# A decoder step on one core: the samples' pages with paired square sums, casts on ScalarE and products with the values four pages at a time

## The chip, the core and the metric

The kernel runs on one core of a Trainium2 chip. Its engines work side by side, each through its own queue of instructions: TensorE (PE in the profile, its weight loads PEld) multiplies matrices into the accumulator memory PSUM; VectorE (DVE), ScalarE (ACT) and GpSimd (POOL) do elementwise work and sums; SyncE (SP) issues transfers. An instruction waits, by semaphores, for what it reads and for the buffer that it writes. The metric is the time of one execution on the device in microseconds (us); lower is better.

## The reference

One step of a one-layer decoder for 512 prompt tokens and 8 samples (one new token each). Attention, a chunk mixer, a convolutional feed-forward part and a gate follow one another; all in fp32. The change touches the samples' attention over the past: 4096 positions for each sample, in 32 pages of 128, found through a page table in a cache of 128-wide latents and 32-wide rope keys. Cut to that:

```python
def keys_nope(c, w_uk, k_norm_w):
    return rmsnorm(jnp.einsum('bkr,rhd->bkhd', c, w_uk), k_norm_w)

def attend(q_nope, q_rope, k_nope, k_rope, c, w_uv, q_pos, k_pos):
    s = (jnp.einsum('bqhd,bkhd->bhqk', q_nope, k_nope)
         + jnp.einsum('bqhd,bkd->bhqk', q_rope, k_rope)).astype(jnp.float32) * SCALE
    s = jnp.where(k_pos[None, :] <= q_pos[:, None], s, -jnp.inf)
    p = jax.nn.softmax(s, axis=-1).astype(c.dtype)
    o_lat = jnp.einsum('bhqk,bkr->bqhr', p, c)
    return jnp.einsum('bqhr,rhd->bqhd', o_lat, w_uv)
```

So the keys of 8 heads are made from each latent and normalised by their own root mean square over 64 values; that is what the sums of squares are for.

## The kernel before, in words

An fp32 product is made of three products of rounded operands: each factor is split into a high part (a cast) and a low part (what the cast left), and `mm3` (L145) issues high by high, high by low, low by high (L146 to L148).

The samples are eight batches, one for each sample, numbered 0 to 7, of 32 pages. Four pages make a group: `s_load_group` (L577) fetches it some groups ahead, with four page transfers on SP's queue (L601) and an indirect transfer of rope keys on POOL (L588). `s_split` (L703) splits a group's latents: the cast (L714, `a<-u` or `a<-w`) runs on ACT for even groups and on DVE for odd ones, the remainder (L130) on POOL.

`s_page` (L718) does one page: six matmuls of 260 columns (256 key values and 4 raw scores, twice) into a pair of PSUM banks, of which there are three pairs. ACT squares the keys out of PSUM into a buffer of 512 (L750, from a pool of three, `Q`) and copies the raw scores (L751), which frees the pair. DVE sums each 64 squares, 512 to 8 values (L752). Every second group, rope scores are made (L740) and copied (L742).

When a batch's last page has been issued, `s_softmax` (L759) appends its steps to a list, and from the fourth page of the next batch on, one step is issued per page: scale the sums (POOL, L792); logarithm, exponential and square on ACT (L770), which give the inverse root y0 and t = y0²; raw scores times y0 (POOL, L796); `newton` on DVE (L157, L158); add (L798); the maximum of each row (L799); TensorE transposes the maxima (`mx_t`, L782); DVE reduces and spreads them (L785, L786); TensorE copies them to all rows (`mx_b`, L789); DVE subtracts (L803); ACT exponentiates; DVE sums (L806). `mx_t` stands in TensorE's queue among the next batch's pages: if the maxima are late, the pages behind it wait.

`s_pv` (L809), after group 5 of the next batch, multiplies the weights with the values: 32 matmuls of 128 columns, page c in column strip c modulo 4 of the array, and one for the new token (L818). `s_out` (L821) copies the result, `s_fin` (L828) adds the strips with a selection matrix and divides by the sum.

The tile framework allots buffers from tagged pools (`U` has 20 buffers of 1040 and `W` 9 of 1024; pages and splits of groups use both, `A` has the split halves) and a scheduler orders each engine's instructions; `tc.issue_after` adds an order. Batch 0's pages run among the prompt's attention blocks, batches 1 to 7 in the loop at L919. In that loop, at group 60 (in batch 7), the prompt's mixer result is split (`split_all`, L931: casts L135 on ACT, remainders L130 `u<-u` on POOL, 128 by 1040). Behind the pages come the output projection and the feed-forward part, which are matmuls with streamed weights.

Of the kernel before, what the change touches and what calls it, by code (L numbers as in the profile page):

```python
# [12 lines left out]
AF = mybir.ActivationFunctionType  # L13
# [9 lines left out]
DN = 64  # L23
# [10 lines left out]
NCONST = 1389  # L34
# [12 lines left out]
def trunk_step(ctx: ExitStack, tc: tile.TileContext, I, O):  # L47
# [68 lines left out]
    sel = take(8)  # L116
    sel_last = take(8)
# [32 lines left out]
    def mm_cols(out, lhsT, rhs):  # L150

        for q in range(0, 128, 32):
            r = nc.tensor.matmul(out[q:q + 32], lhsT[:, q:q + 32], rhs, start=True, stop=True, tile_position=(0, q))  # L153
        return r
# [546 lines left out]
    bst = {}  # L701

    def s_split(n):  # L703
        if n >= 64:
            return
        b, g = n // 8, n % 8
        pv = pages[b][1][g]
        if n < 12:
            t = U(F32R)
            ch, cl = t[:, 0:512], t[:, 512:1024]  # L710
        else:
            ch, cl = A(F32R)[:, 0:512], A(F32R)[:, 0:512]
        raw = pv[:, :, 0:128]
        (nc.vector.tensor_copy if n % 2 else nc.scalar.copy)(u3(ch, 4, 128), raw)  # L714
        subs.append(sub(u3(cl, 4, 128), raw, u3(ch, 4, 128), "g"))
        csp[n] = (ch, cl)

    def s_page(q):  # L718
# [3 lines left out]
        if j == 0:  # L722
            for m in (n + 2, n + 3):
                if m not in csp and (m == n + 2 or m > 12):
                    s_split(m)
            if g == 0:
                ss = up.tile([128, 256], F32, tag="ss", name=nm("ss"), bufs=2)
                raw = up.tile([128, 256], F32, tag="raw", name=nm("raw"), bufs=2)
                sc = up.tile([128, 288], F32, tag="sc", name=nm("sc"), bufs=2)
                nc.gpsimd.memset(sc[:, 264:288], 0.0)  # L730
                nc.vector.tensor_copy(sc[:, 256:264], snall[:, b])
                bst[b] = (ss, raw, sc)
# [16 lines left out]
        sq = Q()  # L749
        squares.append(nc.scalar.activation(u3(sq, 2, 256), ps[:, :, 0:256], AF.Square))  # L750
        nc.scalar.copy(raw[:, c * 8:c * 8 + 8].rearrange("p (a h) -> p a h", a=2), ps[:, :, 256:260])  # L751
        nc.vector.tensor_reduce(ss[:, c * 8:c * 8 + 8], sq.rearrange("p (h d) -> p h d", d=DN), axis=AX.X, op=ALU.add)  # L752
# [6 lines left out]
    def s_softmax(b):  # L759
# [28 lines left out]
        def mx_b():  # L788
# [6 lines left out]
            lambda: act(t, y0, AF.Square),  # L795
# [3 lines left out]
            lambda: nc.vector.tensor_reduce(m1[:, 0:8], s3.rearrange("p c h -> p h c"), axis=AX.X, op=ALU.max),  # L799
            mx_t,  # L800
# [8 lines left out]
    def s_pv(b):  # L809

        scp, psum = bst.pop(b)
        pg = pages.pop(b)[1]
        po = ms()
        for c in range(32):
            q = 32 * (c % 4)
            nc.tensor.matmul(po[q:q + 32, 0:128], scp[:, c * 8:c * 8 + 32], pg[c // 4][:, c % 4, 128:256],  # L816
                             start=(c < 4), stop=(c >= 29), tile_position=(0, q))
        nc.tensor.matmul(po[0:32, 0:128], scp[:8, 256:288], cnew, start=False, stop=True, tile_position=(0, 0))  # L818
        bst[b] = (po, psum)

    def s_out(b):  # L821
        po, psum = bst.pop(b)
        ol = Q()[:, 0:128]
        with tc.issue_after(squares[-1].ins):
            nc.scalar.copy(ol, po[:, 0:128])
# [318 lines left out]
def _layout(inp):  # L1144
# [27 lines left out]
    def col(v):  # L1172
# [14 lines left out]
         np.tile(np.eye(32, 8, dtype=f), (4, 1)), np.tile(np.eye(32, 8, -24, dtype=f), (4, 1))], 1)  # L1187
# [59 lines left out]
```

## Time and profile before

| | |
|---|---|
| time, three runs | 919.24, 922.05, 924.79 us; median 922.05 |
| time of the profiled execution | 920.34 us |
| its span in the profile | 918.6 us |
| mean granted TensorE clock | 0.99 of full speed |
| first square of batch 1 | 206.15 us |
| last square of batch 7 | 420.06 us |

The profile is of one execution. A group row names line, engine, operation, result and source tiles with their shape, count, then busy time and mean ns of one, then idle time ahead of it and what ended that. A timeline row has start, length, engine, line, operation, and in brackets the idle time before it with what ended it. A wait row names who waited, for whom, the total, the count and the longest. A row of a stretch has its length and for each engine busy time and number of instructions, then the granted clock, the share of the DMA engines and GB/s.

### The profile page before, as it was taken

What the parts mean: (1) busy time and instruction counts of PE and PEld (TensorE: products, weight loads), DVE (VectorE), ACT (ScalarE), POOL (GpSimd) and SP (SyncE); (2) the same over time, 40 slices, a digit from 0 to 9 for tenths busy, and PEclk for the clock granted to TensorE, in tenths of its full rate; (3) what the DMA queues carried; (4) which work ended last, traced back from release to release, by engine and by line L of the source; (5) the groups of instructions that cost most, each with busy time, mean ns of one, the idle gap of its engine ahead of it and who ended that gap; (6) DMA issues with size and microseconds to landing.
All of it is one profiled execution on the core that took longest, in us unless ns stands there. A gap on an engine that the chain in (4) does not pass through costs nothing.

```text
span 918.6 us, 20633 instructions
## 1 busy us (share of the span) xinstructions
PE 892.9 (97%) x7799; PEld 846.5 (92%) x7799; DVE 660.2 (72%) x1133; ACT 503.0 (55%) x1188; POOL 204.7 (22%) x208
## 2 busy tenths in 40 slices
PE   7998999999999999989999999999999999999997
PEld 5896878888898888979999999999999999999997
DVE  6579766669999999897668776337776337776775
ACT  6573368777877787864446443224444214455561
POOL 5004841127676667630000000000000000000000
PEclk9998999999999999989999999999999999999999
DMA  6332150352667556314233222322222222323311
GB/s 217 99 96 81 50 182 1 95 161 79 203 183 210 161 162 193 121 31 138 86 100 110 89 86 86 103 89 87 90 93 92 93 92 93 104 85 98 116 58 59
DMA packets 65204, 100.44 MB, mean 109 GB/s; under 512 B 13825, under 2 KB 47754, under 8 KB 65106
## 3 DMA queue, kind: packets, MB, share of 16 engines
q1 hardware_dynamic: 63058, 94.93, 32.3%
q0 software_dynamic: 2048, 4.20, 1.8%
q8 instruction: 62, 1.02, 0.5%
q14 instruction: 36, 0.29, 0.1%
HBM read 95.95 MB, written 3.15 MB: 108 GB/s over the span
## 4 chain that ended last, share of the span: by engine, by line
PE 82%; DVE 7%; ACT 3%; DMA 2%; issue 2%; SPq 2%; POOL 1%; DVEq 0%; ACTq 0%
PE mm L146 24%; PE mm L148 24%; PE mm L147 23%; DVE ss L752 2%; PE ms L816 2%; PE ms L693 2%; SPq L601 1%; POOL xs L280 1%; DMA u<-pages 1%; DVE g L157 1%; DMA a<-xT 1%; PE ms L153 1%; PE mm L678 1%; PE ms L641 1%; PE mm L658 1%
## 5 line engine op out<-in xcount | busy, mean ns | idle before, releaser
L146 PE MATMUL mm<-u,w 128*128 128x260 f32 x1392 | 395.2, 284 | 0.0
L148 PE MATMUL mm<-u,w 128*128 128x260 f32 x1392 | 394.3, 283 | 0.0
L147 PE MATMUL mm<-u,w 128*128 128x260 f32 x1392 | 393.4, 283 | 0.0
L148 PEld LDWEIGHTS mm<-u,w 128*128 128x128 f32 x1392 | 262.0, 188 | 0.3 <-issue 0.2
L147 PEld LDWEIGHTS mm<-u,w 128*128 128x128 f32 x1392 | 262.1, 188 | 0.2
L146 PEld LDWEIGHTS mm<-u,w 128*128 128x128 f32 x1392 | 261.8, 188 | 0.4 <-PE mm L148 0.2
L130 DVE TENSOR_TENSOR w<-wr,w 128x1024 fp32r<-128x1024 f32 (+1 forms) x94 | 112.8, 1201 | 104.2 <-issue 54.3
L752 DVE TENSOR_REDUCE ss<-sq 128x8 f32<-128x512 f32 x256 | 166.6, 679 | 14.1 <-ACT sq L750 12.2
L750 ACT ACTIVATE sq<-mm 128x512 f32<-128x512 f32 x256 | 153.6, 614 | 34.7 <-PE mm L148 21.1
L135 ACT CAST w<-wr 128x1024 fp32r<-128x1024 f32 (+1 forms) x94 | 96.5, 1031 | 138.1 <-PE mm L148 127.3
L146 PE MATMUL mm<-wuk,a 128*128 128x260 f32 x416 | 124.8, 300 | 3.9 <-ACT raw L751 3.4
L148 PE MATMUL mm<-wuk,a 128*128 128x260 f32 x416 | 119.0, 286 | 0.0
L147 PE MATMUL mm<-wuk,a 128*128 128x260 f32 x416 | 118.6, 285 | 0.0
L146 PEld LDWEIGHTS mm<-wuk,a 128*128 128x128 f32 x416 | 79.4, 191 | 7.8 <-ACT raw L751 6.4
L147 PEld LDWEIGHTS mm<-wuk,a 128*128 128x128 f32 x416 | 79.6, 191 | 0.0
L148 PEld LDWEIGHTS mm<-wuk,a 128*128 128x128 f32 x416 | 79.4, 191 | 0.0
L588 POOL DMA_INDIRECT wr<-krT,idx x64 | 62.1, 971 | 11.4 <-issue 6.3
L1059 ACT ACTIVATE a<-abuf,cst 128x512 f32<-128x512 f32 x44 | 35.9, 816 | 39.3 <-DVE abuf L1057 39.2
L1060 DVE SCALAR_TENSOR_TENSOR a<-abuf,cst,a 128x512 f32<-128x512 f32 x44 | 33.1, 752 | 25.4 <-ACT a L1059 25.1
L130 POOL TENSOR_TENSOR a<-u,a 128x512 fp32r<-128x512 f32 x34 | 45.5, 1339 | 25.8 <-ACT a L714 13.0
L751 ACT COPY raw<-mm 128x8 f32<-128x8 f32 x256 | 45.9, 179 | 0.0
L135 ACT CAST u<-a 128x520 fp32r<-128x520 f32 x24 | 14.8, 626 | 43.4 <-DVE a L1098 43.3
(306 smaller groups left out, 1339.3 us busy)
## 6 DMA issues: line engine op xcount, KB each, us to landing
wr<-w_ffi SPq DMA_DIRECT2D x44, 512.0 KB, 3.3
u<-pages SPq DMA_DIRECT2D x152, 128.0 KB, 2.3
w<-pages SPq DMA_DIRECT2D x104, 128.0 KB, 2.4
wr<-w_ffo SPq DMA_DIRECT2D x16, 512.0 KB, 3.3
wr<-w_o SPq DMA_DIRECT2D x8, 512.0 KB, 4.3
wr<-w_pg SPq DMA_DIRECT2D x8, 512.0 KB, 3.2
wr<-w_ffo SPq DMA_DIRECT2D x8, 384.0 KB, 3.4
a<-xT SPq DMA_DIRECT2D x8, 260.0 KB, 7.2
```

Of the source, the lines that this page charges most:

```text
L130: return (nc.vector if eng == "v" else nc.gpsimd).tensor_sub(dl, src, dh.bitcast(F32))
L135: nc.scalar.copy(dh, src)
L146: nc.tensor.matmul(out, lh, rh, start=start, stop=False)
L147: nc.tensor.matmul(out, lh, rl, start=False, stop=False)
L148: return nc.tensor.matmul(out, ll, rh, start=False, stop=stop)
L588: nc.gpsimd.indirect_dma_start(krT[:, g * 128:(g + 1) * 128], None, I["krT"], bass.IndirectOffsetOnAxis(ap=idx.bitcast(U32)[:, b * 8 + g:b ...
L693: nc.tensor.matmul(po[:, 0:256], v[:, ks], pt_[:, k * 256:k * 256 + 256], start=(k == 0), stop=(k == qb))
L750: squares.append(nc.scalar.activation(u3(sq, 2, 256), ps[:, :, 0:256], AF.Square))
L751: nc.scalar.copy(raw[:, c * 8:c * 8 + 8].rearrange("p (a h) -> p a h", a=2), ps[:, :, 256:260])
L752: nc.vector.tensor_reduce(ss[:, c * 8:c * 8 + 8], sq.rearrange("p (h d) -> p h d", d=DN), axis=AX.X, op=ALU.add)
L1059: nc.scalar.activation(c[:, 0:T], a[:, 2:T + 2], AF.Identity, scale=cw[:, m, 2:3], bias=cw[:, m, 3:4])
L1060: nc.vector.scalar_tensor_tensor(c[:, 0:T], a[:, 1:T + 1], cw[:, m, 1:2], c[:, 0:T], op0=ALU.mult, op1=ALU.add)
```

## The change

For batches 1 to 7, the squares of two pages go into the two halves of one `U` buffer, and one reduce sums both, 1024 to 16 values. Batch 0 stays as it was. Casts of all groups from the ninth on (n >= 8) run on ACT. The copy of the new token's score (L731) goes from DVE to POOL, and t = y0² from ACT to a product on POOL. `mx_t` gets one empty step ahead of it. The products with the values take a group of four pages at once, 512 columns with one stationary block of 32 (4 pages by 8 heads), so that the wanted results stand in four diagonal blocks; `s_out` copies all 512 columns, on DVE, and `s_fin` picks the blocks with four selection matrices, 16 matmuls in place of 4. The new token's product moves to the middle. The constants grow from 1389 to 1405 columns.

```diff
-        (nc.vector.tensor_copy if n % 2 else nc.scalar.copy)(u3(ch, 4, 128), raw)
+        (nc.vector.tensor_copy if n % 2 and n < 8 else nc.scalar.copy)(u3(ch, 4, 128), raw)
...
-                nc.vector.tensor_copy(sc[:, 256:264], snall[:, b])
+                nc.gpsimd.tensor_copy(sc[:, 256:264], snall[:, b])
...
-        sq = Q()
+
+        two = b > 0
+        if not two:
+            bsq["t"] = Q()
+        elif j % 2 == 0:
+            bsq["t"] = U()
+        sq = bsq["t"][:, two * (j % 2) * 512:two * (j % 2) * 512 + 512]
...
-        nc.vector.tensor_reduce(ss[:, c * 8:c * 8 + 8], sq.rearrange("p (h d) -> p h d", d=DN), axis=AX.X, op=ALU.add)
+        if not two or j % 2:
+            w = 2 if two else 1
+            nc.vector.tensor_reduce(ss[:, (c + 1 - w) * 8:c * 8 + 8], u3(bsq["t"], 8 * w, DN), axis=AX.X, op=ALU.add)
...
-            lambda: act(t, y0, AF.Square),
+            lambda: nc.gpsimd.tensor_mul(t, y0, y0),
...
             lambda: nc.vector.tensor_reduce(m1[:, 0:8], s3.rearrange("p c h -> p h c"), axis=AX.X, op=ALU.max),
+            None,
             mx_t,
...
-        for c in range(32):
-            q = 32 * (c % 4)
-            nc.tensor.matmul(po[q:q + 32, 0:128], scp[:, c * 8:c * 8 + 32], pg[c // 4][:, c % 4, 128:256],
-                             start=(c < 4), stop=(c >= 29), tile_position=(0, q))
-        nc.tensor.matmul(po[0:32, 0:128], scp[:8, 256:288], cnew, start=False, stop=True, tile_position=(0, 0))
+        for g in range(8):
+            q = 32 * (g % 4)
+            if g == 4:
+                nc.tensor.matmul(po[0:32, 0:128], scp[:8, 256:288], cnew, start=False, stop=False, tile_position=(0, 0))
+            nc.tensor.matmul(po[q:q + 32], scp[:, g * 32:g * 32 + 32], pg[g][:, :, 128:256],
+                             start=(g < 4), stop=(g >= 4), tile_position=(0, q))
...
-        ol = Q()[:, 0:128]
-        with tc.issue_after(squares[-1].ins):
-            nc.scalar.copy(ol, po[:, 0:128])
+        ol = Q()
+        nc.vector.tensor_copy(ol, po)
...
-            mm_cols(pt_[:, 0:8], ol, sel)
+            for j in range(4):
+                mm_cols(pt_[:, 0:8], ol[:, j * 128:j * 128 + 128], sels[j], j == 0, j == 3)
```

The scheduler moves instructions with it. DVE, from the seventh page of batch 4 on (the rows of batch 3's softmax stand between batch 4's reduces; `ss`, `raw`, `sc` are sums, scores and the result). Before:

```order
467 L714 CAST a_4673<-u_4513 128x512
468 L752 TENSOR_REDUCE ss_4531<-sq_4641 128x8
469 L157 SCALAR_TENSOR_TENSOR g_4508<-ss_3910,g_4508 128x256
470 L752 TENSOR_REDUCE ss_4531<-sq_4653 128x8
471 L752 TENSOR_REDUCE ss_4531<-sq_4694 128x8
472 L158 SCALAR_TENSOR_TENSOR raw_3911<-g_4508,raw_3911 128x256
473 L752 TENSOR_REDUCE ss_4531<-sq_4707 128x8
474 L798 TENSOR_TENSOR sc_3912<-sc_3912,raw_3911 128x256
475 L752 TENSOR_REDUCE ss_4531<-sq_4719 128x8
476 L799 TENSOR_REDUCE s_4509<-sc_3912 128x8
```

DVE at the same place, after:

```order
399 L761 TENSOR_REDUCE ss_4399<-u_4481 128x16
400 L157 SCALAR_TENSOR_TENSOR g_4376<-ss_3822,g_4376 128x256
401 L761 TENSOR_REDUCE ss_4399<-u_4503 128x16
402 L158 SCALAR_TENSOR_TENSOR raw_3823<-g_4376,raw_3823 128x256
403 L807 TENSOR_TENSOR sc_3824<-sc_3824,raw_3823 128x256
404 L761 TENSOR_REDUCE ss_4399<-u_4554 128x16
405 L808 TENSOR_REDUCE s_4377<-sc_3824 128x8
```

The cast is gone from between, and from the first newton step to the maximum two paired reduces stand where four single ones stood.

TensorE at the transpose of the maxima in batch 4 (`mm` is a page's PSUM pair, each page six rows). Before:

```order
1746 L146 MATMUL mm_4784<-wuk_563,a_4527 128x260
1747 L147 MATMUL mm_4784<-wuk_564,a_4527 128x260
1748 L148 MATMUL mm_4784<-wuk_563,a_4528 128x260
1749 L782 MATMUL ms_4735<-cst,s_4509 8x128
1750 L146 MATMUL mm_4784<-wuk_563,a_4527 128x260
1751 L147 MATMUL mm_4784<-wuk_564,a_4527 128x260
1752 L148 MATMUL mm_4784<-wuk_563,a_4528 128x260
1753 L146 MATMUL mm_4796<-wuk_563,a_4527 128x260
```

TensorE, after:

```order
1745 L146 MATMUL mm_4625<-wuk_563,a_4395 128x260
1746 L147 MATMUL mm_4625<-wuk_564,a_4395 128x260
1747 L148 MATMUL mm_4625<-wuk_563,a_4396 128x260
1748 L791 MATMUL ms_4623<-cst,s_4377 8x128
1749 L146 MATMUL mm_4637<-wuk_563,a_4395 128x260
1750 L147 MATMUL mm_4637<-wuk_564,a_4395 128x260
1751 L148 MATMUL mm_4637<-wuk_563,a_4396 128x260
```

The transpose stood in the middle of a page, after 14 and a half of batch 4's pages; now it stands after 14.

POOL in batch 7 (`u<-u` rows of 128x1040 are the remainders of the prompt's split, `a<-` rows those of the pages, `raw` the scores of batch 6). Before:

```order
191 L130 TENSOR_TENSOR u_6717<-u_1037,u_6716 128x1040
192 L130 TENSOR_TENSOR a_6470<-w_6297,a_6469 128x512
193 L588 DMA wr_5981<-krT,idx 128x128
194 L796 TENSOR_TENSOR raw_5774<-raw_5774,g_6371 128x256
195 L130 TENSOR_TENSOR a_6537<-u_6376,a_6536 128x512
```

POOL, after:

```order
206 L804 TENSOR_TENSOR g_6107<-g_6107 128x256
207 L805 TENSOR_TENSOR raw_5554<-raw_5554,g_6107 128x256
208 L130 TENSOR_TENSOR a_6265<-u_6112,a_6264 128x512
209 L130 TENSOR_TENSOR a_6323<-u_6187,a_6322 128x512
210 L130 TENSOR_TENSOR a_6373<-w_6250,a_6372 128x512
211 L130 TENSOR_TENSOR u_6429<-u_1036,u_6428 128x1040
212 L130 TENSOR_TENSOR u_6433<-u_1037,u_6432 128x1040
```

Both remainders of the prompt's split now stand behind the scores and behind the last remainder of a page; t stands ahead of the scores.

More of the change, by code (lines that the diff above doesn't have):

```diff
@@ L33 @@
 EPS = 1e-6
-NCONST = 1389
+NCONST = 1405
 NEG = -1.0e30
@@ L115, in trunk_step @@
     row8 = take(272)
-    sel = take(8)
-    sel_last = take(8)
+    sels = [take(8) for _ in range(4)]
+    sel, sel_last = sels[0], sels[3]
     gqk8 = row8[:8, 0:128].rearrange("p (a d) -> p a d", a=2)
@@ L148, in mm3, with mm_cols @@
         return nc.tensor.matmul(out, ll, rh, start=False, stop=stop)
-    def mm_cols(out, lhsT, rhs):
+    def mm_cols(out, lhsT, rhs, start=True, stop=True):
         for q in range(0, 128, 32):
-            r = nc.tensor.matmul(out[q:q + 32], lhsT[:, q:q + 32], rhs, start=True, stop=True, tile_position=(0, q))
+            r = nc.tensor.matmul(out[q:q + 32], lhsT[:, q:q + 32], rhs, start=start, stop=stop, tile_position=(0, q))
         return r
@@ L701, in trunk_step @@
     bst = {}
+    bsq = {}
     def s_split(n):
@@ L1186, in _layout @@
          np.where(np.tril(np.ones((128, 128))) > 0, 0.0, NEG).astype(f), cw.reshape(128, 176), row8,
-         np.tile(np.eye(32, 8, dtype=f), (4, 1)), np.tile(np.eye(32, 8, -24, dtype=f), (4, 1))], 1)
+         *(np.tile(np.eye(32, 8, -8 * j, dtype=f), (4, 1)) for j in range(4))], 1)
     a["pt"] = g["page_table"].reshape(1, 256)
```

## The prediction

> **What bounds the kernel now.** The page's busy table first: it gives engine, busy time, share of the span.
>
> ```profile
> PE 892.9 (97%) x7799; PEld 846.5 (92%) x7799; DVE 660.2 (72%) x1133; ACT 503.0 (55%) x1188; POOL 204.7 (22%) x208
> ```
>
> TensorE is the bound over the whole span, so an edit that only lightens DVE gains where TensorE waits for DVE. The change touches the samples' pages; batches 1 to 7 run from about 206 to 421 us. I cut that stretch at each batch's first square and asked for busy time in each part (columns: length, then PE, PEld, DVE, ACT, POOL busy, granted clock, DMA share, GB/s). Batch 4 stands for batches 1 to 6, which differ little; the last row is batch 7 with what follows it.
>
> ```profile
> 295.48:325.40 29.92, 28.88 (x343) 26.80 (x342) 27.51 (x50) 23.59 (x78) 19.69 (x20) 1.00 0.58 172
> ...
> 385.27:437.00 51.73, 47.51 (x514) 44.16 (x513) 41.97 (x69) 32.15 (x88) 14.76 (x18) 0.93 0.25 86
> ```
>
> In batch 4 TensorE idles 29.92 - 28.88 = 1.04 us, while DVE is busy 27.51 of 29.92: DVE runs almost level with TensorE. Next, batches 4 and 7 cut at the transpose of the row maxima (L782, which belongs to the batch before) and at the last square.
>
> ```profile
> 295.48:307.19 11.71, 10.67 (x97) 9.86 (x96) 11.40 (x20) 10.34 (x33) 9.48 (x9) 1.00 0.71 210
> 307.19:324.81 17.62, 17.62 (x241) 16.35 (x242) 15.52 (x30) 13.06 (x45) 10.10 (x10) 1.00 0.49 147
> 385.27:400.28 15.01, 11.38 (x101) 10.38 (x99) 13.91 (x19) 12.10 (x37) 12.14 (x13) 1.00 0.25 83
> 400.28:420.66 20.38, 20.38 (x228) 19.09 (x229) 17.66 (x30) 14.15 (x44) 1.48 (x3) 0.83 0.24 83
> ```
>
> All of batch 4's idle time lies ahead of the transpose (10.67 of 11.71; behind it 17.62 of 17.62), where DVE is busy 11.40 of 11.71. Batch 7 takes 15.01 to the same place, 3.3 more, and then 20.38 against 17.62, 2.8 more, at a mean clock of 0.83. Shorter windows show the fall:
>
> ```profile
> 398.00:401.00 3.00, 0.78 (x7) 0.73 (x7) 3.00 (x5) 2.10 (x6) 0.81 (x1) 1.00 0.00 0
> 401.00:404.00 3.00, 3.00 (x28) 2.47 (x28) 1.92 (x5) 1.80 (x7) 0.00 (x0) 0.50 0.00 0
> 404.00:407.00 3.00, 3.00 (x14) 2.98 (x15) 2.54 (x6) 1.20 (x6) 0.96 (x1) 0.50 0.00 0
> ```
>
> TensorE is busy 0.78 of 3 us while it waits for the maxima; then the lower of its two levels (1.2 GHz) is granted for over 6 us. Last, the waits by pair, for PEld from 205 to 440 us and for ACT from 204 to 424 us (total, times, longest):
>
> ```profile
> PEld ms L782 <- DVE s L799: 8.3, 8, 2.4
> PEld mm L146 <- ACT raw L751: 6.4, 12, 1.4
> ```
>
> ```profile
> ACT sq L750 <- DVE ss L752: 9.6, 13, 1.5
> ```
>
> TensorE waits for the maxima from DVE, and for ACT's copies of scores. ACT in turn waits for DVE's reduces to free one of three square buffers. Both waits come from DVE's queue.
>
> **The change, part by part.** The costs of single operations, from the groups between 204 and 424 us (busy and mean ns of one stand behind the bar):
>
> ```profile
> L752 DVE TENSOR_REDUCE ss<-sq 128x8 f32<-128x512 f32 x226 | 146.8, 679 | 10.9 <-ACT sq L750 9.0
> L714 DVE CAST a<-u 128x512 fp32r<-128x512 f32 x14 | 12.6, 898 | 0.0
> L731 DVE COPY sc<-snall 128x8 f32<-128x8 f32 x6 | 6.2, 1031 | 2.9 <-PE ms L818 2.9
> L714 ACT CAST a<-u 128x512 fp32r<-128x512 f32 x20 | 12.7, 636 | 0.0
> L770 ACT ACTIVATE g<-g 128x256 f32<-128x256 f32 x16 | 7.7, 480 | 0.1
> L825 ACT COPY sq<-ms 128x128 f32<-128x128 f32 x7 | 2.0, 286 | 0.0
> L816 PE MATMUL ms<-u,sc 128*32 128x128 f32 x264 | 10.3, 275 | 0.0
> L816 PE MATMUL ms<-w,sc 128*32 128x128 f32 x184 | 8.0, 273 | 0.0
> ```
>
> The chain from batch 3's squares to its transpose, in batch 4, by the timeline: first POOL and ACT, then DVE, then two matmuls of the page behind the transpose (which starts at 307.19).
>
> ```profile
> 299.78 1.00 POOL L588 DMA_INDIRECT wr<-krT,idx  x1 [0.15 <-issue]
> 300.79 0.75 POOL L796 TENSOR_TENSOR raw<-raw,g 128x256 f32<-128x256 f32 x1
> 301.97 1.31 POOL L130 TENSOR_TENSOR a<-u,a 128x512 fp32r<-128x512 f32 x1 [0.43 <-PE mm L148]
> ```
>
> ```profile
> 300.00 0.47 ACT L770 ACTIVATE g<-g 128x256 f32<-128x256 f32 x1
> ```
>
> ```profile
> 300.74 1.10 DVE L714 CAST a<-u 128x512 fp32r<-128x512 f32 x1
> 301.76 0.67 DVE L752 TENSOR_REDUCE ss<-sq 128x8 f32<-128x512 f32 x1
> 302.35 1.21 DVE L157 SCALAR_TENSOR_TENSOR g<-ss,g 128x256 f32<-128x256 f32 x1
> 303.48 1.27 DVE L752 TENSOR_REDUCE ss<-sq 128x8 f32<-128x512 f32 x2
> 304.67 0.41 DVE L158 SCALAR_TENSOR_TENSOR raw<-g,raw 128x256 f32<-128x256 f32 x1
> ...
> 306.53 0.61 DVE L799 TENSOR_REDUCE s<-sc 128x8 f32<-128x264 f32 x1
> ```
>
> ```profile
> 307.43 0.28 PE L147 MATMUL mm<-wuk,a 128*128 128x260 f32 x1
> 307.55 0.28 PE L148 MATMUL mm<-wuk,a 128*128 128x260 f32 x1
> ```
>
> *Paired squares.* Sixteen reduces of 1024 replace 32 of 512 per batch. Two single ones in a row took 1.27. No row has one of 1024: twice the single is at most 1.27; at least about 0.8, by the step from L799's 0.61 for 264 elements to 0.67 for 512. I take 1.2, nearest to the pair. That frees little by itself; what it brings is room, since the squares leave the three-buffer pool for the 20 buffers of U, and ACT's wait of 9.6 in all goes.
>
> *Casts on ACT.* The 28 that leave DVE in batches 1 to 7 cost it about 0.9 each, 3.6 per batch; ACT pays 0.636 each, 2.5 per batch, and gives back 0.48 (the Square) and 0.29 (the output copy). ACT goes from 23.6 busy per batch to about 25.4 of some 29.3, so it stays hidden behind TensorE. The copy of the new key's score (1.03) leaves DVE for POOL; POOL is busy 19.7 of 29.9, and nobody waits for it there.
>
> *t on POOL.* The Exp ends at 300.47, but POOL is in its indirect DMA until 300.78 and starts t then. At the price of its neighbour, 0.75, t is ready at 301.53 and the scaled scores at 302.28, 0.74 later than before. Behind them POOL's cast remainders (L130) and its next indirect DMAs are queued; the pages use those a group later.
>
> *DVE's chain.* Without the cast and the reduce that filled DVE from 300.74 to 302.35, the first newton step can start at 301.6. At its row's 1.21, since POOL is multiplying beside it, it would end at 302.8; unstretched it would end near 302.2; I take 302.6. A pair reduce follows (303.8), then newton's second step and the addition, 0.41 each by L158's row (304.6), one pair reduce (305.8) and the maximum (306.4). Before, the maximum ended at 307.14, so this is 0.74 earlier. The transpose stands half a page earlier in TensorE's order, so half a page, three matmuls at 0.12 from start to start (0.36), must still be run behind it. That leaves 0.38. I add 0.27, an estimate, for DVE's backlog that no longer follows behind the transpose (11.40 busy of 11.71 there): 0.65 per batch, 3.9 over batches 1 to 6. Bounds: 0 (newton at its longest and reduces at 1.27) to 2.0, the whole wait of TensorE there (of the first rival's 14.7, the 12.3 left when the longest, 2.4 in batch 7, is taken off, over six batches).
>
> The Trainium skill, "SBUF — State Buffer", section "Who interferes with whom", says that a DVE instruction with two SBUF inputs contends with a GpSimd instruction that reads SBUF, while a reduce does not. By it newton beside POOL's two products would be drawn out, and the casts taken off DVE were drawn out the same way. The trace agrees: 1.21 for newton beside the subtraction, 0.67 for every reduce. Were the rule to let newton start only once POOL's products are through, the sum would be that of the second rival.
>
> *Products with the values.* Eight matmuls of 512 columns replace 32 of 128: the same columns stream. Over seven batches the 448 records (two for each of 32) are busy at most 10.3 + 8.0 = 18.3, 2.6 per batch, where 64 of 0.275 one after another would take 17.6: the four strips already overlap. I count 0, from -0.3 (fewer starts) to +0.3; the sixteen selections, 12 more, go with it. The output copy of 512 on DVE (about 0.6 at a reduce's price) lies behind the chain, and its reader is three pages later.
>
> *Batch 7.* Four rows:
>
> ```profile
> 391.05 2.67 DVE L714 CAST a<-u 128x512 fp32r<-128x512 f32 x1
> ```
>
> ```profile
> 389.75 2.43 POOL L130 TENSOR_TENSOR u<-u,u 128x1040 fp32r<-128x1040 f32 x1
> 394.56 0.98 POOL L796 TENSOR_TENSOR raw<-raw,g 128x256 f32<-128x256 f32 x1
> ```
>
> ```profile
> 400.28 0.27 PE L782 MATMUL ms<-cst,s 128*8 128x128 f32 x1 [2.22 <-DVE s L799]
> ```
>
> POOL's 2.43 of the prompt's own split stands ahead of the scores, and the cast on DVE lasts 2.67. The cast goes to ACT, and the order puts the two splits behind all the pages' work on POOL. Then batch 7 should run like batch 4: 3.3 to the transpose, and with the idle stretch the clock's fall goes too, 2.8. Together 6.1; bounds 1 (the clock falls all the same) to 7. The two splits are late for the output projection after the pages, which waits for nothing on POOL before about 421.
>
> Sum: 3.9 + 6.1 = 10.0. The profiled execution took 920.34 (span 918.6), 1.7 under the median of the three runs, 922.05. So 910.3 against the former, and **912.0** against the median.
>
> **The rivals.**
>
> *All waits go* (chance 0.13). If the paired reduces cost near 0.8, or newton isn't drawn out, the maxima come before TensorE asks. PEld's waits in the table, 8.3 + 6.4 = 14.7, vanish, and with them at least 3.0 of lost clock (half speed from 401 to 407): -17.7, 904.4. For it: DVE loses about 7 of 27.5 per batch. Against it: the chain is a series of operations that depend on each other, and POOL's two products stand in it before DVE can help.
>
> *The chain starts later* (0.17). If newton's two inputs make it wait out POOL's products and the subtraction behind them (1.31), each transpose comes 1.3 later than forecast: +0.65 per batch in place of -0.65, +3.9; batch 7 keeps 4.8. Sum -0.9: 921.1. For it: newton's stretch to 1.21 and t's added 0.75. Against: DVE has half its queue to catch up with.
>
> *ACT becomes the bound* (0.06), the slower side. ACT gets 28 x 0.636 = 17.8 and gives back 7 x (0.48 + 0.29) = 5.4. It decides if ACT has no slack between squares: a cast between two squares then holds the copy that frees the PSUM pair, and TensorE waits at a page's start. At full price, +12.4, without the steady gain and with batch 7's 6.1: +6.3, 928.4. For it: TensorE already waits 6.4 for that copy. Against: ACT is busy 23.6 of 29.9, and three PSUM pairs absorb one cast of 0.64.
>
> *Batch 7 still stalls* (0.12). ACT now casts the prompt's splits too; if its squares get late there and the clock falls again, 1 of the 6.1 remains: -4.9, 917.2.
>
> **How the numbers follow.** The forecast has 0.52. About 0.5% (4.6 us) is what a measurement of this kernel can tell from no change. Faster by more than that: forecast, the first rival, and half of the last, which sits on the line (917.4): 0.71. Within: the second rival and the other half, 0.23. Slower: ACT, 0.06. The range, 903 to 921, takes in the first rival, the bounds of the steady term and the last rival; it leaves out ACT's case and about half of the second rival.
>
> **What would show it.** In the profile after: no wait of ACT's squares for DVE; DVE busy near 21 per batch; batches 1 to 6 at about 29.2; the transpose some 11.0 behind the first square in batch 7 as in batch 4; granted clock 1.00 from 400 to 410; reduces of 1024 near 1.2. Wrong if the transpose's wait for DVE is as long as before (second rival), if TensorE's waits for ACT's copies grow (third), or if batch 7 still takes 15 us to its transpose.

## The result, and the profile after

| | before | changed |
|---|---|---|
| median of 9 runs | 920.97 us | 925.49 us |
| lowest to highest | 919.24 to 924.79 | 922.38 to 930.29 |
| ratio to before, 95% interval | | 1.0046 [1.0029, 1.0062] |
| span of the profiled execution | 918.6 | 928.5 |

The change made the kernel slower by half a per cent. A second timing of the same kernel gave 1.0020 [1.0005, 1.0035]. The profiled execution of the changed kernel is the longest of its nine; a second profile (below, e_repeat) has a span of 918.4. So the parts that both profiles show are the kernel's, and the part that only one shows is marked.

The batches of the changed kernel, each from its first square to the next one's, the last from batch 7's first square on (length, then PE, PEld, DVE, ACT, POOL busy, granted clock, DMA share, GB/s):

```profile
208.38:242.75 34.37, 31.17 (x319) 28.11 (x318) 22.92 (x29) 25.46 (x80) 22.29 (x24) 0.90 0.49 143
242.75:280.33 37.58, 34.19 (x319) 29.82 (x318) 26.36 (x30) 25.26 (x81) 20.02 (x22) 0.86 0.43 124
...
310.60:340.82 30.22, 28.78 (x319) 25.82 (x318) 24.86 (x30) 24.47 (x80) 20.09 (x22) 1.00 0.52 154
...
401.31:453.00 51.69, 48.98 (x502) 43.43 (x501) 43.35 (x56) 34.67 (x89) 17.59 (x17) 1.00 0.41 137
```

Batches 1 and 2 are 34.37 and 37.58 long, against 29.47 and 29.87 before, and the clock's mean in them is 0.90 and 0.86. Batches 3 to 6 take 30.2 to 30.3 each, where they took 29.9 to 30.0 and 29.3 was forecast. In batch 7 the clock no longer falls: 1.00 where 0.93 stood; from its first to its last square it takes 29.2 where it took 34.8. The difference of the two spans, +9.9, by parts: 2.2 late at batch 1's first square, +4.9 in batch 1, +7.7 in batch 2, +1.2 in batches 3 to 6 together, -5.6 in batch 7, -0.5 behind. The first 2.2 are not in the second profile, whose batch 1 starts at 205.40.

What TensorE's weight loads wait for in the whole span of the changed kernel:

```profile
PEld ms L791 <- DVE s L808: 10.6, 8, 3.6
...
PEld ms L828 <- issue: 6.7, 8, 0.8
...
PEld ms L798 <- DVE s L795: 4.5, 5, 0.9
PEld mm L146 <- ACT raw L758: 3.5, 3, 2.3
```

The wait for the maxima is longer than before (10.6 against 8.3), and behind it stands one that was not there: L798, the copy of the maximum to all rows, waits for DVE's spread L795. The 0.8 ahead of each of the eight products of the new token (L828), now in the middle of the others, is idle time of the weight load alone: TensorE's own waits have no such row. The wait for ACT's score copies has almost halved (6.4 before).

Batch 4 of the changed kernel, cut at the transpose of the maxima and at the copy of the maximum to all rows (columns as above):

```profile
310.60:321.12 10.52, 9.80 (x95) 9.41 (x93) 9.32 (x11) 10.38 (x35) 9.30 (x10) 1.00 0.53 158
321.12:324.92 3.80, 3.08 (x36) 2.69 (x36) 3.77 (x5) 2.60 (x10) 2.24 (x2) 1.00 0.40 119
```

TensorE idles 0.72 ahead of the transpose, where it idled 1.04 before: 0.32 less. Between the transpose and the copy it idles another 0.72, where it had no idle time before. The timeline shows why. Before, DVE and then PE from the maximum's end (307.14) on:

```profile
307.06 1.26 DVE L752 TENSOR_REDUCE ss<-sq 128x8 f32<-128x512 f32 x2
308.25 0.27 DVE L785 TENSOR_REDUCE s<-ms 8x1 f32<-8x128 f32 x1
...
309.04 0.21 DVE L786 TENSOR_SCALAR s<-cst,s 8x8 f32<-8x8 f32 x1
```

```profile
309.66 0.38 PE L789 MATMUL ms<-s,ones 8*128 8x8 f32 x2
```

The changed kernel, DVE:

```profile
316.53 0.94 DVE L157 SCALAR_TENSOR_TENSOR g<-ss,g 128x256 f32<-128x256 f32 x1
317.40 1.21 DVE L761 TENSOR_REDUCE ss<-u 128x16 f32<-128x1024 f32 x1
...
320.44 0.62 DVE L808 TENSOR_REDUCE s<-sc 128x8 f32<-128x264 f32 x1
320.98 2.34 DVE L761 TENSOR_REDUCE ss<-u 128x16 f32<-128x1024 f32 x2
323.23 0.27 DVE L794 TENSOR_REDUCE s<-ms 8x1 f32<-8x128 f32 x1
323.54 1.33 DVE L795 TENSOR_SCALAR s<-cst,s 8x8 f32<-8x8 f32 x1
```

POOL and PE at the end of that stretch:

```profile
323.57 1.28 POOL L130 TENSOR_TENSOR a<-w,a 128x512 fp32r<-128x512 f32 x1 [1.35 <-ACT a L715]
```

```profile
324.92 0.38 PE L798 MATMUL ms<-s,ones 8*128 8x8 f32 x2 [0.72 <-DVE s L795]
```

The maximum (L808) ends at 321.06, 10.46 behind the batch's first square at 310.60; before, it ended 11.66 behind. So the chain up to there gained 1.2. Then two paired reduces of 2.34 together stand ahead of the maximum's second reduce (L794), where two single ones of 1.26 stood; it starts 12.63 behind the first square, against 12.77 before. And the spread, an operation on 8 by 8 elements, takes 1.33 where it took 0.21: it ends with POOL's subtraction, which began beside it and took 1.28. The copy to all rows starts at 324.92, 14.32 behind the first square against 14.18 before. All of the 1.2 is gone.

Batch 2 of the changed kernel, where newton is longest: POOL, then DVE, then PE.

```profile
249.22 0.75 POOL L805 TENSOR_TENSOR raw<-raw,g 128x256 f32<-128x256 f32 x1
249.92 1.29 POOL L130 TENSOR_TENSOR a<-u,a 128x512 fp32r<-128x512 f32 x1
```

```profile
249.31 2.20 DVE L157 SCALAR_TENSOR_TENSOR g<-ss,g 128x256 f32<-128x256 f32 x1 [0.60 <-POOL g L804]
251.43 1.21 DVE L761 TENSOR_REDUCE ss<-u 128x16 f32<-128x1024 f32 x1
252.56 1.48 DVE L158 SCALAR_TENSOR_TENSOR raw<-g,raw 128x256 f32<-128x256 f32 x1
```

```profile
256.21 0.38 PE L791 MATMUL ms<-cst,s 128*8 128x128 f32 x1 [3.39 <-DVE s L808]
```

Newton starts beside POOL's second product and ends 0.30 behind the subtraction that follows it without a gap (249.92 + 1.29 = 251.21). Its second step meets the next subtraction and takes 1.48, where it took 0.41 in batch 4. TensorE waits 3.39 ahead of the transpose. In batch 4 newton starts beside the same product; but there POOL pauses 0.16 ahead of the subtraction, and newton takes 0.94. This holds in every profile of this case: all eight newtons beside a product that a subtraction followed without a gap took 2.15 to 2.20, and all those where the gap was 0.06 to 0.18 took 0.94 to 0.95. The granted clock around it:

```profile
254.00:258.00 4.00, 1.79 (x8) 1.49 (x9) 3.97 (x7) 1.72 (x6) 0.88 (x1) 0.71 0.76 228
258.00:262.00 4.00, 4.00 (x30) 3.47 (x29) 1.96 (x3) 2.08 (x8) 1.28 (x1) 0.50 0.13 41
```

TensorE is busy 1.79 of 4 us, and then the lower level is granted: what batch 7 did before, batch 2 does now.

Last, what SP's page loads wait for between 180 and 290 us, before, and then in the changed kernel:

```profile
SPq L601 <- PE ms L816: 23.1, 2, 16.7
```

```profile
SPq L601 <- DVE ss L761: 17.5, 5, 7.6
```

A load waits for the buffer that it is to fill. Before, the longest of these waits were for the products that read the old pages; now the most is for paired reduces, since squares take buffers of U, which pages need.

### The profile page after: what moved, and what is told of

Its sections match the earlier page's. It is cut to its first block, busy times and chain, and to the rows that moved or that the text cites. A ratio compares the mean times of both kernels' runs of the same rounds, so it can differ in the third digit from the quotient of the medians.

```text
span 928.5 us, 20082 instructions
## 1 busy us (share of the span) xinstructions
PE 897.3 (97%) x7607; PEld 840.5 (91%) x7607; DVE 642.9 (69%) x993; ACT 510.8 (55%) x1200; POOL 210.8 (23%) x224
## 3 DMA queue, kind: packets, MB, share of 16 engines
q1 hardware_dynamic: 63058, 94.93, 32.6%
## 4 chain that ended last, share of the span: by engine, by line
PE 79%; DVE 9%; ACT 5%; DMA 2%; issue 2%; POOL 1%; SPq 1%; ACTq 0%; DVEq 0%
PE mm L146 23%; PE mm L148 22%; PE mm L147 22%; DVE ss L761 4%; ACT u L757 2%; PE ms L693 2%; PE ms L829 2%; POOL xs L280 1%; DVE g L157 1%; DMA a<-xT 1%; DVE w L130 1%; PE ms L146 1%; DVE s L795 1%; ACT wr L666 1%; PE mm L678 1%
## 5 line engine op out<-in xcount | busy, mean ns | idle before, releaser
L761 DVE TENSOR_REDUCE ss<-u 128x16 f32<-128x1024 f32 x112 | 135.4, 1214 | 38.3 <-ACT u L757 33.7
L757 ACT ACTIVATE u<-mm 128x512 f32<-128x512 f32 x224 | 132.6, 620 | 29.9 <-PE mm L148 12.7
L146 PEld LDWEIGHTS mm<-wuk,a 128*128 128x128 f32 x416 | 80.9, 194 | 2.7 <-ACT raw L758 1.2
L147 PEld LDWEIGHTS mm<-wuk,a 128*128 128x128 f32 x416 | 81.0, 195 | 0.1
L148 PEld LDWEIGHTS mm<-wuk,a 128*128 128x128 f32 x416 | 80.8, 194 | 0.0
L1072 DVE SCALAR_TENSOR_TENSOR a<-abuf,cst,a 128x512 f32<-128x512 f32 x44 | 33.1, 751 | 25.7 <-ACT a L1071 25.4
```

The source lines that it names most:

```text
L146: nc.tensor.matmul(out, lh, rh, start=start, stop=False)
L147: nc.tensor.matmul(out, lh, rl, start=False, stop=False)
L148: return nc.tensor.matmul(out, ll, rh, start=False, stop=stop)
L761: nc.vector.tensor_reduce(ss[:, (c + 1 - w) * 8:c * 8 + 8], u3(bsq["t"], 8 * w, DN), axis=AX.X, op=ALU.add)
L1072: nc.vector.scalar_tensor_tensor(c[:, 0:T], a[:, 1:T + 1], cw[:, m, 1:2], c[:, 0:T], op0=ALU.mult, op1=ALU.add)
```

## The experiments

Ratios are to the kernel before, timed together with the run on the same chip. The kernel before itself differs by up to 4 us from one such timing to the next (medians of 917.3 to 921.7), so ratios are what is compared. Each length of a batch is from the profile of that run, first square to first square (batch 7: to its last square).

| run | ratio, 95% interval | batch 1 | batch 2 | batches 3 to 6 | batch 7 |
|---|---|---|---|---|---|
| before | 1 | 29.5 | 29.9 | 29.9 to 30.0 | 34.8 |
| changed | 1.0046 [1.0029, 1.0062] | 34.4 | 37.6 | 30.2 to 30.3 | 29.2 |
| e_repeat | 1.0020 [1.0005, 1.0035] | 30.3 | 34.9 | 30.1 to 30.2 | 29.2 |
| e_spread_act | 0.9990 [0.9973, 1.0007] | 30.5 | 36.4 | 29.4 | 28.5 |
| e_old_pv | 1.0076 [1.0052, 1.0101] | 29.9 | 33.1 | 29.9 to 30.0 | 29.7 |
| e_casts_only | 0.9941 [0.9920, 0.9962] | 30.2 | 29.5 | 29.5 to 30.0 | 29.1 |
| e_t_act | 0.9944 [0.9925, 0.9963] | 33.9 | 30.6 | 29.3 | 28.6 |
| e_no_casts | 1.0182 [1.0150, 1.0214] | 36.3 | 33.9 | 31.6 to 33.1 | 31.0 |
| e_no_pairs | 1.0050 [1.0033, 1.0066] | 31.6 | 30.3 | 30.3 to 30.8 | 35.4 |
| e_best | 0.9948 [0.9931, 0.9965] | 34.5 | 30.4 | 29.0 | 29.2 |
| e_casts_t | 0.9956 [0.9936, 0.9975] | 31.2 | 29.5 | 29.5 to 30.0 | 32.6 |
| e_pairs_only | 0.9948 [0.9929, 0.9967] | 32.5 | 31.2 | 29.8 | 28.1 |
| e_best_b2 | 0.9907 [0.9880, 0.9934] | 31.6 | 29.7 | 29.0 | 29.2 |
| e_best_b3 | 0.9919 [0.9888, 0.9950] | 31.5 | 29.5 | 29.0 | 29.2 |
| e_own_sq | 1.0041 [1.0021, 1.0061] | 30.5 | 29.3 | 30.2 | 34.4 |
| e_best_own | 0.9902 [0.9873, 0.9932] | 29.7 | 28.9 | 28.9 to 29.5 | 28.5 |

**e_repeat.** The changed kernel, no edit.

> The changed kernel once more, for a second profile. In the first, batches 1 and 2 took 34.4 and 37.6 us against 29.5 and 29.9 before, with TensorE idle about 3 us in each and the clock then at half; batches 3 to 6 took 30.2, batch 7 29.2 to its last square against 34.8. If the stalls of batches 1 and 2 belong to the program (the order of its instructions), they come again: 34 and 37, and the time is 924 to 929. If they are accidents of one execution, batches 1 and 2 take about 30.2 as the others, and this profile's time is near 918.

```profile
205.40:235.66 30.26, 28.99 (x319) 25.72 (x318) 22.70 (x29) 25.13 (x81) 22.36 (x24) 1.00 0.53 163
235.66:270.55 34.89, 31.48 (x319) 27.33 (x318) 26.22 (x30) 25.25 (x80) 20.02 (x22) 0.95 0.45 134
```

Batch 2's stall comes again and so belongs to the program; batch 1's does not come again. In batch 1 of the first profile the clock falls at about 221.6, in a stretch in which TensorE waits 2.25 for ACT's copy of scores. ACT itself had stood still from 217.92 to 222.16 ahead of a copy of rope scores (L743); the profile names TensorE's L798 as what it waited for, but that had ended at 220.74, so what held ACT is not known. A fall between 217 and 222 shows in the profiles of e_t_act, e_best, e_no_casts and e_pairs_only too, and not in those of e_spread_act and e_old_pv. All of these keep batch 1's squares in U; no kernel that doesn't has a fall there. Why one execution has it and another not stays open.

**e_spread_act.**

```diff
-            nc.vector.tensor_scalar(m2[:8, 8:16], ident[:8, 0:8], m2[:8, 0:1], None, op0=ALU.mult)
+            nc.scalar.activation(m2[:8, 8:16], ident[:8, 0:8], AF.Copy, scale=m2[:8, 0:1])
```

> The changed kernel, with the spread of the maximum (8x8) on ACT in place of DVE. Theory A: from batch 3 on the transpose comes 1.2 us earlier than before, but the gain is lost again at the copy of the maximum to all rows, because DVE's spread takes 1.33 us in place of 0.21 while POOL subtracts; then TensorE's wait there (4.5 us in all) goes to under 1.5, batches 3 to 6 take 29.5 to 29.8 in place of 30.2, and the time falls by 2 to 4 against the changed kernel. Rival B: DVE's two paired reduces ahead of the maximum's reduce make it late, and the spread hides in that: batches stay at 30.1 or more, time within 1 us.

Batch 4 and, from its timeline, ACT's spread:

```profile
300.75:330.12 29.37, 28.63 (x319) 25.69 (x318) 23.63 (x29) 24.91 (x82) 20.17 (x22) 1.00 0.54 161
```

```profile
313.96 0.28 ACT L795 ACTIVATE s<-cst,s 8x8 f32<-8x8 f32 x1
```

The spread takes 0.28, TensorE's wait at L798 goes from 4.9 in the repeat to 0.6 in all, and batches 3 to 6 fall by 0.8 each, batch 7 by 0.7. The ratio falls by 0.003 against the repeat, which was timed together with it: some 3 us. Theory A, with its size. The Trainium skill, "SBUF — State Buffer", section "Who interferes with whom", has the rule that fits: a tensor_scalar can enter a mode that takes the port pair which VectorE and GpSimd share, whoever issues first keeps it for the whole instruction, and the other is blocked, not slowed. The trace agrees on the length: 1.33 on DVE, ending with POOL's 1.28. Which of the two issued first it does not settle, since DVE's record starts 0.03 earlier. In e_no_pairs POOL's record starts 0.17 earlier, and the spread again ends with it, after 1.13.

**e_old_pv.** `s_pv`, `s_out` and the selection of `s_fin` as before (the diff is that of the change, backwards).

> The changed kernel with products, copy and selection as before (33 matmuls of 128 columns, ACT's copy of 128, 4 selections); squares, casts and the rest changed. Theory A: products and selection cost 0.3 us of TensorE per batch (2.31 against 2.22, and 12 more selections), so batches take 0.3 less, the time falls by 2 to 2.5, and the stalls of batches 1 and 2 stay. Rival C: DVE's copy of 512 and the later selection stand in the way of the next batch's chain, and batches fall by 0.6 or more, or batches 1 and 2 lose their stalls: 5 to 10 less.

```profile
296.15:326.09 29.94, 28.51 (x343) 26.79 (x342) 24.04 (x29) 24.90 (x82) 20.11 (x22) 1.00 0.54 163
```

Batches 3 to 6 take 0.2 to 0.3 less, as theory A has it, and batch 2 keeps its stall (33.1). But five of its six runs took 923 to 927, and the ratio is above the repeat's. The profiled execution was the sixth, 918.3, so its profile does not show where the others lost their time. That stays open.

**e_casts_only.** The kernel before with one line of the change:

```diff
-        (nc.vector.tensor_copy if n % 2 else nc.scalar.copy)(u3(ch, 4, 128), raw)
+        (nc.vector.tensor_copy if n % 2 and n < 8 else nc.scalar.copy)(u3(ch, 4, 128), raw)
```

> The kernel before with only the casts of all groups from the ninth on moved to ACT. Theory A: batch 7's gain comes from the casts alone (the 2.67 us cast leaves DVE, POOL's splits of the prompt move behind); batch 7 falls from 34.8 to 30 or less, and batches 1 to 6 stay or fall a little since newton is no longer behind a cast: 912 to 916. Rival D: it needed the paired reduces as well, because ACT with its casts now waits for DVE to free square buffers: batch 7 over 32, batches 1 to 6 over 30: 919 or more.

```profile
293.25:322.95 29.70, 29.08 (x343) 26.85 (x342) 25.63 (x46) 25.29 (x83) 19.71 (x20) 1.00 0.56 165
...
382.52:411.62 29.10, 28.18 (x321) 25.90 (x320) 26.14 (x43) 25.88 (x80) 12.35 (x15) 1.00 0.29 96
```

Batch 7 loses 5.7 us and the clock stays up; batches 2 to 6 fall by 0.2 on the mean, and batch 1 rises by 0.7. One line gives 0.6%: the rest of the change took more than that back.

**e_t_act.**

```diff
-            lambda: nc.gpsimd.tensor_mul(t, y0, y0),
+            lambda: act(t, y0, AF.Square),
```

> The changed kernel with t made by ACT's Square again, one product less on POOL. In every profile of the changed kernel batch 2 takes 33 to 38 us, with newton at 2.2 us (0.95 in batch 3), the transpose 3.4 us late and the clock then at half. Theory A: POOL's two products and the subtraction right behind them hold newton off; with one product less, newton starts before or behind them as in batch 3, batch 2 takes about 30.2 and the time falls by 4 to 6. Rival B: the subtraction alone, coming earlier, meets newton all the same: batch 2 over 33, and other batches may join it; no gain.

Batches 2 and 4, and newton in batch 4:

```profile
242.24:272.83 30.59, 29.98 (x319) 25.90 (x318) 23.71 (x30) 25.28 (x81) 19.73 (x21) 1.00 0.53 152
...
302.18:331.50 29.32, 29.01 (x319) 25.92 (x318) 23.53 (x30) 24.83 (x81) 19.54 (x21) 1.00 0.58 164
```

```profile
308.14 0.42 DVE L157 SCALAR_TENSOR_TENSOR g<-ss,g 128x256 f32<-128x256 f32 x1
308.67 0.42 DVE L158 SCALAR_TENSOR_TENSOR raw<-g,raw 128x256 f32<-128x256 f32 x1
```

Newton is 0.42 in batch 4, where it was 0.94, and 0.89 in batch 2, where it was 2.20; batch 2's stall is gone, and batches 3 to 6 fall by 0.9. The ratio falls by 0.008 to 0.010, 7 to 9 us, more than expected: with POOL's work shifted by one product, the spread no longer meets a subtraction either (L798 waits 0.4 in all), so this 0.9 and the 0.8 of e_spread_act are in the main the same wait. Theory A for batch 2. Batch 1 has the stall of the first profile (33.9).

**e_no_casts.** The line of e_casts_only taken back in the changed kernel.

> The changed kernel with the casts of odd groups back on DVE. Theory A: batch 7's gain (29.2 against 34.8) is the casts' alone; it goes back to 33 or more, since one cast on DVE then lasts over 2 us beside POOL's splits, and batches 3 to 6 rise from 30.2 to 30.5 or more: 4 to 8 slower than the changed kernel. Rival B: the paired reduces give DVE the room to bear the casts: batch 7 stays under 31 and the time within 2.

It is 1.4 to 1.6% slower than the changed kernel, 13 to 15 us: batches 3 to 6 rise to 31.6 and more, batch 7 only to 31.0. The harm is larger than expected, and it lies in all batches rather than in batch 7: in batches 3 to 6 TensorE waits 2.0 ahead of the transpose, against 0.7 in the changed kernel. No cast on DVE lasts over 1.1 in batches 1 to 7, where I expected one of over 2, so theory A's cause did not come.

**e_no_pairs.**

```diff
-        two = b > 0
+        two = False
```

> The changed kernel with one reduce per page in the three-buffer pool again; casts, t, copies and products as changed. Theory A: two paired reduces ahead of the maximum's second reduce and the missing reduce between it and the spread are what make the copy of the maximum late; with single reduces TensorE's wait there (4.5 to 4.9 in all) vanishes, batches 3 to 6 take 29.8 or less, near the casts-only kernel (29.5 to 30.0) plus 0.3 for the products. Batch 2: if t on POOL is the cause of its stall, it stays over 33; if the pairs are, it goes: 30.

```profile
297.18:327.48 30.30, 29.03 (x319) 25.78 (x318) 26.19 (x46) 24.97 (x80) 20.45 (x22) 1.00 0.59 174
...
388.62:424.02 35.40, 31.89 (x297) 27.64 (x296) 28.09 (x46) 26.11 (x79) 13.08 (x15) 0.90 0.28 95
```

Batch 2 runs without a stall (30.3), so the pairs have a part in it. But batches 3 to 6 don't fall, L798 still waits 3.5 us in all, and batch 7's stall is back. My expectation for the steady batches failed: the pairs are not what makes the copy of the maximum late. With single reduces the spread still takes 1.13 beside POOL's subtraction.

**e_best.** e_old_pv, e_t_act and e_spread_act together.

> Paired squares and all casts on ACT as changed, with t on ACT, the spread of the maximum on ACT and the products, copy and selection as before. If the costs found add up (0.75 per batch from the spread, 0.25 from the products, batch 2's stall from t), batches take 29.2 and batch 7 28.5: 906 to 909, below the casts-only kernel (about 912). If batch 2 still stalls, 911 to 914.

Batches 3 to 6 take 29.0, a little under the 29.2 expected, and batch 7 29.2, where 28.5 was expected. But batch 1 stalls in the profile (34.5), and the ratio of 0.9948 is no better than that of the casts alone: the 906 to 909 us that I expected did not come.

**e_casts_t.** e_casts_only with `nc.gpsimd.tensor_mul(t, y0, y0)` for ACT's Square.

> The casts-only kernel with t made on POOL, nothing else. Theory A: t on POOL is what harms: newton on DVE, which reads two operands from SBUF, starts while POOL runs its two products and meets the subtraction behind them; newton goes from 0.41 to 0.95 or 2.2, batches 1 to 6 rise from 29.5-30.0 to 30.2 or more, batch 7 may fall back into its stall (35): 4 to 10 slower than the casts-only kernel, no longer faster than before. Rival B: t on POOL harms only beside paired reduces; within 2 of the casts-only kernel, 0.994 of before.

DVE and POOL in batch 7:

```profile
390.85 2.16 DVE L157 SCALAR_TENSOR_TENSOR g<-ss,g 128x256 f32<-128x256 f32 x1 [2.15 <-POOL g L795]
```

```profile
390.76 0.75 POOL L796 TENSOR_TENSOR raw<-raw,g 128x256 f32<-128x256 f32 x1
391.45 1.27 POOL L130 TENSOR_TENSOR a<-u,a 128x512 fp32r<-128x512 f32 x1
```

In batch 7 newton waits 2.15 for t and then lasts until the product and the subtraction are through, 2.16; the batch goes back to 32.6. Batches 2 to 6 stay at 29.5 to 30.0 with newton at 0.95, so the harm that I expected there did not come. The ratio of 0.9956 lies within the interval of the casts alone: by it, t on POOL costs 1 or 2 us here, less than the two intervals can tell from nothing, and not 4 to 10.

This kernel and e_no_pairs differ in the products, the empty step ahead of `mx_t` and the copy on POOL. The spread takes 0.21 here and 1.13 there, and batches 3 to 6 take some 0.8 less here, of which the products are 0.25 by e_old_pv. No run takes the empty step or the copy alone, so which of them put the spread beside POOL's subtraction stays open.

**e_pairs_only.** The kernel before with the squares' edit of the change alone.

> The kernel before with only the squares of two pages summed at once. Theory A: the pairs free ACT of its wait for square buffers but leave the cast in DVE's chain and batch 7's stall as they were: batches 1 to 6 at 29.5 to 30.2, batch 7 34 or more, ratio 0.995 to 1.005. Rival B: the room on DVE alone gives most of the gain: batch 7 under 31, ratio under 0.993.

```profile
205.33:237.84 32.51, 30.20 (x343) 28.20 (x342) 24.36 (x32) 23.49 (x77) 20.80 (x21) 0.95 0.52 150
...
388.04:416.17 28.13, 28.03 (x321) 25.96 (x320) 26.54 (x31) 26.08 (x78) 15.47 (x12) 1.00 0.42 129
```

The pairs alone heal batch 7 too (28.1) and cost 3.0 and 1.3 in batches 1 and 2. The ratio, 0.9948, is at the lower end of what theory A had; the place is rival B's.

**e_best_b2, e_best_b3.** e_best with `two = b > 1` and `two = b > 2`.

> The kernel with pairs, casts on ACT, t and spread on ACT and the old products, with pairs from batch 2 on only. In its run with pairs from batch 1 on, batch 1 took 34.5 (clock at half from 217 on) and batch 2 30.4, the others 29.0. If pairs in batch 1 make its stall, batch 1 takes 30.2 or less: 4 less, ratio 0.990 to 0.992. If the stall is of another cause, it comes again: no change.

> The same with pairs from batch 3 on only. Batches 1 and 2 then run as in the casts-only kernel (30.2 and 29.5), batches 3 to 6 at 29.0, batch 7 at 29: 2 to 3 less than the casts-only kernel, ratio 0.990 to 0.992. If batch 2 wants pairs, it takes over 30 and the ratio is 0.993 or more.

Both reach 0.991 to 0.992, though the interval of e_best_b3 overlaps that of the casts alone. Without pairs batch 1 takes 31.5, batch 2 with pairs 29.7, without 29.5. Batch 1 is over the 30.2 that I expected in both, so not all of its loss is the pairs'.

**e_own_sq.** The squares get their own buffers, and pages keep U to themselves.

```diff
-    def Q(dt=F32):
+    def Q(dt=F32, w=512):
-        return up.tile([128, 512], dt, tag="sq", name=nm("sq"), bufs=3)
+        return up.tile([128, 1024], dt, tag="sq", name=nm("sq"), bufs=2)[:, 0:w]
...
-            bsq["t"] = U()
+            bsq["t"] = Q(w=1024)
...
-        ol = Q()
+        ol = G()[:, 0:512]
```

> The changed kernel with paired squares in the square pool (two buffers of 1024 in place of three of 512, used by all its users; the output copy goes to another pool), so that pages keep U to themselves. Theory A: late page loads in batches 1 and 2 come from the sharing; SP no longer waits for the paired reduces, batch 1 takes 30.2 and batch 2 30.2 as batches 3 to 6, and the time falls by 4 to 6, ratio 0.996 to 0.999. Rival B: batch 2's stall is the lock of newton alone: it takes 33 or more again. Two buffers may also hold ACT, then batches 3 to 6 rise over 30.5.

```profile
204.21:234.69 30.48, 29.71 (x319) 25.84 (x318) 22.75 (x29) 25.17 (x80) 22.48 (x24) 1.00 0.42 122
234.69:264.01 29.32, 28.60 (x319) 25.71 (x318) 23.83 (x30) 24.96 (x80) 20.13 (x22) 1.00 0.56 164
...
384.75:419.18 34.43, 30.84 (x297) 26.67 (x296) 26.75 (x29) 26.04 (x78) 13.37 (x15) 0.95 0.29 98
```

What SP waits for from 180 to 290 us:

```profile
SPq L601 <- PE ms L829: 15.2, 1, 15.2
```

SP no longer waits for DVE's reduces, and batch 2 takes 29.3 with newton at 0.94: without the sharing of U batch 2 does not stall. It takes 0.9 less than batches 3 to 6, since there the spread takes 0.22. (The edit also leaves two square buffers in place of three, which costs batches 3 to 6 nothing: 30.2 as before.) But now batch 7 stalls:

```profile
388.56 2.43 POOL L130 TENSOR_TENSOR u<-u,u 128x1040 fp32r<-128x1040 f32 x1
```

POOL's split of the prompt stands ahead of t again, newton waits 2.60 for t and then takes 2.16, and the ratio stays at 1.0041. Theory A for batches 1 and 2; the gain was lost in batch 7, where newton is drawn out in the same way.

**e_best_own.** e_best with the squares in their own buffers.

> Pairs in the square pool, all casts, t and the spread of the maximum on ACT, the old products. Theory A: batches 1 and 2 at 29.5 or less (34.5 and 30.4 with the squares in U), batches 3 to 6 at 29.0: ratio 0.988 to 0.991. Rival B: batch 1 over 31 again, ratio 0.992 or more.

```profile
205.89:235.54 29.65, 29.35 (x343) 27.14 (x342) 21.49 (x27) 25.32 (x82) 21.84 (x23) 1.00 0.37 105
...
293.41:322.36 28.95, 28.63 (x343) 26.79 (x342) 22.58 (x28) 25.51 (x84) 19.57 (x21) 1.00 0.63 183
...
380.76:409.28 28.52, 28.10 (x326) 26.22 (x325) 24.51 (x27) 25.93 (x81) 12.73 (x15) 1.00 0.31 96
```

No batch stalls: 28.9 to 29.7, batch 7 28.5. Median 908.92 against 918.21 before, timed together with it, 0.9902 [0.9873, 0.9932]: faster than the kernel before and the changed one.

## Why the prediction was wrong, step by step

**What bounds the kernel.** Right: TensorE is busy 97% in both, and what moves the time is where it waits, mostly for DVE.

**Paired squares, the price.** Right: 1.21 in the row above against 1.2. What DVE is spared I had too high: it is busy 24.9 in batch 4 where I said 21. Single reduces in a row start every 0.60, less than their length of 0.68; batch 4's four casts had taken 2.4 and not 3.6, since my 0.9 for each was the mean of half of them (the others took 0.42); and the spread is 1.1 longer and the output copy new.

**DVE's chain.** Right up to the transpose. The maximum came 1.2 earlier and not 0.74, since newton ended 6.9 behind the first square (7.1 forecast) and what follows starts up to 0.1 earlier than the rows' lengths say. TensorE's idle time ahead of the transpose fell by 0.32 (0.38 forecast). Wrong behind it. The step that failed is "I add 0.27, an estimate, for DVE's backlog that no longer follows behind the transpose". The prediction's own row has TensorE busy 17.62 of 17.62 there, so there was nothing to gain. In place of +0.27 stands a loss of 0.72: TensorE waits for the copy of the maximum, because the spread meets POOL's subtraction and takes 1.33. e_spread_act moves the spread to ACT, and batches 3 to 6 get 0.8 back. The two paired reduces ahead of it, which look like the cause in the timeline, are not enough to explain it: e_no_pairs has single ones, and TensorE still waits 0.5 there in each of batches 3 to 6. I followed the chain to the transpose and stopped there, though the front part lists DVE's reduce and spread and TensorE's copy behind it.

**Products.** Taken at 0 between -0.3 and +0.3: they cost 0.25, at the edge of the range (e_old_pv's batches 3 to 6; the ratio of that run does not bear it out).

**Batches 1 to 6 by batch 4.** The step that cost most: "Batch 4 stands for batches 1 to 6, which differ little." They did before. The squares went from a pool of their own into one that page loads use, and I counted that as "room". It made page loads wait, 17.5 us in all; in batch 2 POOL's work then fell so that newton ended only behind two POOL operations and its second step only behind a third. Batch 2 lost 5.0 to 7.7 us by it where 0.65 was to be gained. e_own_sq takes the sharing away, and batch 2 falls to 29.3; e_t_act keeps it but makes t on ACT, and batch 2 falls to 30.6. So the stall needs both. The second rival had this mechanism, newton waiting out POOL's product and the subtraction behind it, with 1.3 for each batch; it came in one batch, with 3.4 of TensorE's waiting and a fall of the clock behind it, while in batches 3 to 6 newton, with the gap of 0.16 on POOL behind the product, took 0.94.

**Batch 7.** Right: 5.6 against 6.1, the transpose at 10.5 behind the first square and the clock at 1.00. e_casts_only shows that the casts alone do it, and e_pairs_only that the pairs alone do it as well. What the two share is the order on POOL, which the prediction named: in the kernels whose batch 7 takes over 34 (before, e_no_pairs, e_own_sq) a split of the prompt of 2.4 stands 3.6 to 4.5 behind the batch's first square, ahead of the scores; in the changed kernel, e_casts_only and e_pairs_only none starts between the first square and 13.8 behind it. No run changes that order alone. The stall of the fourth rival did not come in the changed kernel, but in e_own_sq and e_no_pairs, and in part in e_casts_t; there it was newton waiting for t and being drawn out, not ACT's squares.

**Casts on ACT.** Right: the third rival (ACT as the bound) is refuted by e_casts_only, 0.9941, with ACT busy 25.3 of 29.7, where I had 25.4. That the measured 925.5 lies nearest to this rival's 928.4 is chance.

**The signs.** Of the 10 us of the sum, 5.6 came, those of batch 7. Batches 3 to 6 lost 1.2 together where they should have gained 2.6, batch 2 lost 7.7 in the first profile and 5.0 in the second, and batch 1 lost 4.9 and 0.8, of which the larger stays unexplained. ACT's wait for DVE's reduces did not go altogether: 9.6 became 4.1, in two places.

## What to carry to other kernels

Follow a chain across engines to its last step, not to the first wait that it removes: here a step behind the transpose, of 0.21 before, took 1.33 beside another engine's work, and TensorE lost more there (0.72) than it had gained ahead of the transpose (0.32). A buffer pool that an edit starts to share is part of the edit: ask which transfer waits for that pool. And an operation that is moved to GpSimd isn't hidden by GpSimd's idle time alone; look at what VectorE does with two SBUF operands, or with a tensor_scalar or a cast, beside it and beside what GpSimd does next.

## What the runs showed of the hardware

- A DVE instruction with two SBUF operands (newton) took 0.42, 0.94 or 2.2 us for the same 128x256 elements: without a POOL product beside it, beside one with a gap of 0.16 behind it, and beside one with a subtraction right behind. In the last case it ended 0.3 behind the second POOL instruction (batch 2 of the changed kernel).
- A tensor_scalar of 8x8 elements took 1.33 beside a POOL subtraction of 1.28, 0.21 with no POOL instruction beside it, and 0.28 as an ACT instruction. In e_own_sq it took 1.35 where the subtraction's record began 0.05 behind its own (batches 3 to 6), and 0.22 where it began 0.06 behind (batch 2).
- A reduce of 1024 elements took 1.21 against 0.68 for 512; from start to start 1.13 (2.34 for two) against 0.60, so pairing saves 0.07 per pair.
- TensorE's wait of 3.4 us ahead of the transpose in batch 2 was followed by half the granted clock in the first profile of the changed kernel, as the wait of 2.2 in batch 7 was before; in e_old_pv's batch 2, with the same wait of 3.4, the clock stayed at 1.00. What decides between the two is not shown here.
